# Moving the rests of w_up's pairs from POOL to DVE, a wide unit 13, the last norm's rows made twice, and the second tile of x on ACT's queue

## The chip, the core and the metric

The kernel runs on one core of a Trainium2 chip. The core has five engines with instruction streams of their own: TensorE (PE: matrix products, with weight loads shown apart as PEld), VectorE (DVE), ScalarE (ACT), GpSimd (POOL) and SyncE (SP, which here only issues transfers). They work from SBUF (on-chip memory) and PSUM (the banks into which PE writes) and wait for one another by semaphores. The metric is the device time of one launch in microseconds, as the median of several runs. The kernel before takes 1517.14 us (three runs, 1516.60 to 1517.77).

## The reference, cut to what matters

A decoder trunk of two layers on 512 tokens of 1024 channels. Each layer has a norm, one wide projection, two attention mixers, an output projection, a second norm and a squared-ReLU MLP; a final norm follows the last layer. The change lies in the MLP's first product, in the very first norm's input, and in the final norm.

```python
def rmsnorm(x, g):
    xf = x.astype(jnp.float32)
    y = xf * lax.rsqrt(jnp.mean(xf * xf, axis=-1, keepdims=True) + RMS_EPS)
    return (y * g.astype(jnp.float32)).astype(x.dtype)

def hybrid_layer(x, norm_mix, w_in, ..., norm_mlp, w_up, w_down):
    h = rmsnorm(x, norm_mix)
    proj = h @ w_in
    ...
    x = x + mixed @ w_out
    h = rmsnorm(x, norm_mlp)
    return x + jnp.square(jax.nn.relu(h @ w_up)) @ w_down

def reference(x, ..., norm_final):
    for l in range(DEPTH):
        x = hybrid_layer(x, ...)
    return rmsnorm(x, norm_final)
```

All is float32, with D_MODEL = 1024, SEQ = 512, D_FF = 4096.

## The kernel before

**Precision.** Each operand of a product is kept as a pair: a part `h` in the type fp32r, made by a copy on ACT, and a rest `lo = value - h`, a subtraction (TENSOR_TENSOR) that DVE or POOL makes. A product is then three matmuls: h by h, h by rest, rest by h (lines 243 to 245, and in the same way 358 to 360 in the first projection, 1529 ff. and 1543 ff. in the MLP). The channels lie on the 128 partitions and the tokens along the free dimension, so x is eight tiles `x[0]` to `x[7]` of 128 x 512.

**The head.** `token_proj` (line 332) takes x tile by tile as it arrives. `first_u` (1197) issues the load of tile k and makes `u` from it: `make_u` (265) scales the tile by the norm's gain on ACT (line 268) and takes the rest on DVE (269). `sumsq` (272) squares the tile on ACT (279) and adds it to a running sum `acc` on POOL, the last one on DVE (289). The weights wva are split by `convert` (ACT line 217, DVE line 218). `rstd` (296) then sums over the partitions with PE (303), takes the reciprocal root in a few small steps (306 to 318) and spreads the result over all partitions with PE again (323), from where it is copied to SBUF (327). A table load (ACT_TABLE_LOAD, line 294) stands before the last square.

**The MLP.** `mlp` (1087) makes eight of w_up's 32 column blocks plainly (`PLAIN`); the other 24 go in twelve units g = 4 to 15, a pair of column blocks each, by a scheme of Strassen's kind with seven products for four rows and columns of blocks (`unit`, 1547). A unit makes its products one after another into PSUM banks. Between them `next(conv, None)` converts the next unit's operands (ACT line 1521, DVE line 1522; sums of weights on DVE at 1517 and 1519, and by accumulating transfers that POOL issues at 1494 and 1503), and `between()` puts in a `down` (1104): four steps of w_down's product (twelve matmuls, 243 to 245), which DVE adds to x (1108). The seven results are combined by ACT copies (1606 to 1616) and by DVE (1620, 1624, 1628), and `halves` (1637) adds two halves on DVE (1640). `act` (1643) makes the activation of each of the unit's two blocks: relu and square on ACT (1652, 1653), its fp32r part on ACT (1654), and its rest (1655), on POOL for all but the last two of each layer's blocks. PE waits for the results of all of these: a bank can be filled again only when its reader has taken it (1108, 1628 and others), and a `down` reads activations.

A unit's products are made wide or slim. In the wide form (`product`, 1537) x's two parts stand beside each other, so the first matmul of each step has a moving side of 512 columns and the second one of 256; in the slim form (`narrow`, 1526) there are three matmuls of 256. Units 13 to 15 are slim. A slim unit also skips `halves`: it combines its results at 1587, 1591 and 1595.

**The tail.** The last product is followed by `out` (1165), once for each half of the tokens. The second half has nothing behind it: `rstd`, then eight products of x with the spread-out row, six on DVE (from PSUM) and two on POOL (from the copy R in SBUF), in the order written in `write`, and their stores on SP's queue or, for POOL's two, on ACT's.

**What sets the order.** Each engine runs its own stream in order. The program text gives the dependencies and the interleaving shown above; the order of instructions within an engine's stream is settled when the program is built, and it can shift with a small edit. A wait at the head of a stream holds all that stands behind it.

Of the kernel before, what the change touches and what calls it, by code (L numbers as in the profile page):

```python
# [11 lines left out]
F32 = mybir.dt.float32  # L12
F32R = mybir.dt.float32r
AF = mybir.ActivationFunctionType
OP = mybir.AluOpType
# [128 lines left out]
class Body:  # L144
# [151 lines left out]
    def rstd(self, acc, tags=("O", "O"), wait=iter(()), exp=True, copy=True, R=None):  # L296

        nc = self.nc
        n = acc[0].shape[-1] // 128
        ps = self.p(tags[0])  # L300
        for i, t in enumerate(acc):
            for b in range(n):
                nc.tensor.matmul(ps[:, 2 * b:2 * b + 2], t[:, b * 128:(b + 1) * 128], self.ones2,
                                 start=i == 0 and b == 0, stop=i == len(acc) - 1, skip_group_check=True)
        v, s, y, z = (self.t("s4", [128, NB], name=k)[:, :n] for k in "vsyz")
        nc.vector.tensor_scalar(v, ps[:, 0:2 * n:2], 1.0 / D, 1e-6, op0=OP.mult, op1=OP.add)
        if not copy:

            for _ in range(3):
                nc.tensor.matmul(ps[:, 128:256], v[:, :1].to_broadcast([128, 128]), self.ident, start=True, stop=True)  # L310
        nc.scalar.activation(s, v, AF.Sqrt)
        if exp:
            self.table(AF.Exp, s)
        nc.vector.reciprocal(y, s)
        nc.vector.tensor_mul(z, y, y)
        nc.vector.scalar_tensor_tensor(z, z, -0.5, v, op0=OP.mult, op1=OP.mult)
        rc = self.t("g4", [128, NB], name="rcol")[:, :n]
        nc.vector.scalar_tensor_tensor(rc, z, 1.5, y, op0=OP.add, op1=OP.mult)
        for _ in range(2):
            next(wait, None)  # L320
        ps = self.p(tags[1])[:, :128 * n]
        for b in range(n):
            nc.tensor.matmul(ps[:, b * 128:(b + 1) * 128], rc[:, b:b + 1].to_broadcast([128, 128]), self.ident,
                             start=True, stop=True)
        if R is None:
            R = self.t("r", [128, T], name="R")[:, :128 * n]
        nc.scalar.copy(R, ps)
        return (R, rc) if copy else (ps, R)

# [755 lines left out]
    def mlp(self, l, x, u, acc, gm):  # L1087
# [35 lines left out]
        for j in range(self.PLAIN):  # L1123
            ps = self.bank()
            w = self.weights(a["wup"][l, j].rearrange("p k c -> p (k c)"))
            run(self.gemm(ps, w, 0, u))
            if R is None and j == 0:
                pend.append(ps)
                continue
            if R is None:  # L1130
                R, _ = self.rstd(acc, (self.turn_tag(), self.turn_tag()))
                prep = S.prepare(R)
                for p in pend:
                    act(p)
            act(ps)
            for _ in range(3):
                next(prep, None)
# [27 lines left out]
    def out(self, x, f, acc, wait):  # L1165

        nc, a = self.nc, self.a
        n = T // 2
        tags = [self.turn_tag() for _ in range(2)]
        R, r = self.rstd(acc, tags, wait=wait, exp=False, copy=f == 0)  # L1170

        def write():

            for k, w in ((0, 2), (6, 1), (2, 2), (7, 1), (4, 1), (5, 1)):
                y = self.t("t2", [128, 2, n], name="y")[:, :w]
                for j in range(w):
                    pool = f and k > 5
                    (nc.gpsimd if pool else nc.vector).tensor_tensor(
                        y[:, j], x[k + j][:, f * n:(f + 1) * n], r if pool else R, op=OP.mult)
                    if j + 1 < w:  # L1180
                        yield
                (nc.scalar if f and k > 5 else nc.sync).dma_start(a["yT"][f, :, k:k + w], y)
                yield

        return write()
# [10 lines left out]

    def first_u(self, u, k):
        x = self.x0[:, k]
        self.nc.sync.dma_start(x, self.a["xT"][k])
        u.append(self.make_u(x, self.gain[:, :8], k))  # L1200
        return x

# [33 lines left out]
class Strassen:  # L1236
# [310 lines left out]
    def unit(self, g, D, n, acts):  # L1547
        b, nc = self.b, self.nc
        V, A = nc.vector, nc.scalar
        conv = self.convert(g + 1)  # L1550
        places = iter({1: (1,), 2: (0, 1), 3: (0, 1, 2), 4: (0, 1, 2, 3)}.get(n, ()))
        place = [next(places, None)]
        here = iter(range(4))

        def between():
            if next(here) == place[0]:
                place[0] = next(places, None)
                next(D)()

        slim = g > 12  # L1560

        def product(i, onto=None):
            ps = (b.bank()[:, :256] if slim else b.bank()) if onto is None else onto
            (self.narrow if slim else self.product)(ps, g, i, onto is None)
            return ps

        tag = "kd" if g > 13 else "o2"
        if slim:
            m = product(0)
            z = b.t("zc", [128, 2, 512], name="z")  # L1570
            lo, hi = slice(0, 256), slice(256, 512)
            A.copy(z[:, 1, lo], m)
            next(conv, None)
            p5 = product(1)
            A.copy(z[:, 0, hi], p5)
            next(conv, None)
            between()
            product(2, m)
            A.activation(z[:, 1, hi], m, AF.Copy, scale=-1.0)
            next(conv, None)  # L1580
            p4 = product(3)
            A.copy(z[:, 0, lo], p4)
            next(conv, None)
            between()
            product(4, m)
            v = z[:, 0].rearrange("p (k c) -> p k c", k=2)
            V.tensor_tensor(v, v, m[:, None, :].to_broadcast([128, 2, 256]), op=OP.add)
            self.act(z[:, 0], acts, tag)
            next(conv, None)
            p2 = product(5)  # L1590
            V.tensor_tensor(z[:, 1, lo], p2, z[:, 1, lo], op=OP.subtract)
            next(conv, None)
            between()
            product(6, p5)
            V.tensor_tensor(z[:, 1, hi], z[:, 1, hi], p5, op=OP.subtract)
            self.c.append(z)
            self.act(z[:, 1], acts, tag)
            next(conv, None)
            between()
            for _ in conv:  # L1600
                pass
            return
        m = product(0)
        y = b.t("zz", [128, 2, 512], name="y")
        z = b.t("zz" if g < 12 else "zc", [128, 2, 512], name="z")
        A.copy(y[:, 0], m)
        next(conv, None)
        p5 = product(1)
        A.copy(z[:, 1], p5)
        next(conv, None)  # L1610
        between()
        product(2, m)
        A.activation(y[:, 1], m, AF.Copy, scale=-1.0)
        next(conv, None)
        p4 = product(3)
        A.copy(z[:, 0], p4)
        next(conv, None)
        between()
        product(4, m)
        V.tensor_tensor(z, z, m[:, None, :].to_broadcast([128, 2, 512]), op=OP.add)  # L1620
        self.act(self.halves(z, z[:, 0]), acts, tag)
        next(conv, None)
        p2 = product(5)
        V.tensor_tensor(y[:, 0], p2, y[:, 0], op=OP.subtract)
        next(conv, None)
        between()
        product(6, p5)
        V.tensor_tensor(y[:, 1], y[:, 1], p5, op=OP.subtract)
        if g > 11:
            self.c.append(z)  # L1630
        self.act(self.halves(y, y[:, 0] if g < 12 else z[:, 1]), acts, tag)
        next(conv, None)
        between()
        for _ in conv:
            pass
# [7 lines left out]
    def act(self, c, acts, tag):  # L1643

        b, nc = self.b, self.nc
        if tag == "kd":
            if len(acts) % 2 == 0:
                self.late = b.t("kd" if len(acts) == 30 else "a4", [128, 4, T], F32R, name="ohl")
            h, lo = (self.late[:, len(acts) % 2 * 2 + i] for i in range(2))
        else:  # L1650
            h, lo = b.two(tag, "o")
        nc.scalar.activation(c, c, AF.Relu)
        nc.scalar.activation(c, c, AF.Square)
        nc.scalar.copy(h, c)
        (nc.vector if len(acts) > 29 else nc.gpsimd).tensor_tensor(lo, c, h.bitcast(F32), op=OP.subtract)  # L1655
        acts.append((h, lo))


# [34 lines left out]
```

## Time and profile before

| | |
|---|---|
| median of three runs | 1517.14 us |
| profiled execution, its own time | 1516.51 us |
| its span in the profile | 1514.7 us |
| granted TensorE clock, mean | 0.998 |
| POOL busy | 190.2 us |
| where w_up's units run (span) | 490 to 720 us and 1240 to 1470 us |

All times in the profile are microseconds from the start of the span, or ns where that is said. A group's row names the line of the kernel, the engine, the operation, what is written and read (buffer numbers left out) with shapes and types, and the count; "[0.52 <-POOL o L1655]" behind a row means that the engine had stood idle for 0.52 us before it, and that POOL's instruction at line 1655 on a tile `o` ended the wait. `ps_S`, `ps_O`, `ps_mm` and `ps_PT` are PSUM banks. Matmuls are pipelined: a row's duration includes the tail that overlaps the next one, so the distance between starts, not the duration, is what one costs.

### The profile page before, as it was taken

To read this page: it belongs to the slowest core of one execution; us is meant where nothing else is said; L and a number is where in the kernel's file an instruction comes from. 1 tells how busy PE (TensorE), PEld (TensorE's weight loads), DVE (VectorE), ACT (ScalarE), POOL (GpSimd) and SP (SyncE) were. 2 spreads that over 40 slices of the span, in tenths; PEclk is the share of its full clock that TensorE was granted. 3 is DMA by queue.
4 is the path that set the end of the run, shared out by engine and by line. 5 is a ranking of instruction groups with operands and counts; after the bars stand their busy time and mean duration, and the time that the engine had idled before them with its cause. 6 is when DMAs were issued, how large, how long until landed. Compare 5 with 4: busy or idle time off the path is not lost.

```text
span 1514.7 us, 22040 instructions
## 1 busy us (share of the span) xinstructions
PE 1500.4 (99%) x7970; PEld 1271.5 (84%) x7970; DVE 1153.3 (76%) x2211; ACT 835.9 (55%) x1592; POOL 190.2 (13%) x195
## 2 busy tenths in 40 slices
PE   9999999999999999999999999999999999999998
PEld 8888888888888888889988788888888888888997
DVE  5678978777478777878846789787674978888785
ACT  6465656554454656555545556565544635656555
POOL 4010000000300222221220000000012002222211
PEclk9999999999999999999999999999999999999999
DMA  7654422227325454553266543222363245555422
GB/s 262 173 164 127 142 70 70 70 70 234 109 96 146 130 149 133 146 143 122 84 197 181 154 125 99 84 70 71 123 205 98 88 142 153 150 141 141 126 77 64
DMA packets 70461, 194.12 MB, mean 128 GB/s; under 512 B 8880, under 2 KB 10288, under 8 KB 70352
## 3 DMA queue, kind: packets, MB, share of 16 engines
q1 hardware_dynamic: 57248, 169.36, 36.1%
q0 software_dynamic: 9216, 16.78, 6.4%
q10 hardware_dynamic: 3888, 6.58, 1.2%
q8 instruction: 63, 1.03, 0.3%
q14 instruction: 46, 0.38, 0.1%
HBM read 148.58 MB, written 4.19 MB: 101 GB/s over the span
## 4 chain that ended last, share of the span: by engine, by line
PE 89%; DVE 5%; ACT 2%; issue 2%; POOL 0%; DMA 0%; SPq 0%; DVEq 0%; ACTq 0%; POOLq 0%
PE ps_mm L243 11%; PE ps_mm L244 11%; PE ps_mm L245 11%; PE ps_PT L243 3%; PE ps_PT L244 3%; PE ps_PT L245 3%; PE ps_O L1543 3%; PE ps_S L1543 3%; PE ps_O L602 2%; PE ps_PT L576 2%; PE ps_S L243 2%; PE ps_S L244 2%; PE ps_S L245 2%; PE ps_S L551 2%; PE ps_O L243 2%; PE ps_O L244 2%
## 5 line engine op out<-in xcount | busy, mean ns | idle before, releaser
L217 ACT CAST wh<-raw 128x1024 fp32r<-128x1024 f32 (+2 forms) x177 | 182.0, 1028 | 238.1 <-PE ps_mm L244 75.8
L218 DVE TENSOR_TENSOR wl<-raw,wh 128x1024 fp32r<-128x1024 f32 (+2 forms) x177 | 218.0, 1232 | 38.1 <-ACT wh L217 37.6
L243 PE MATMUL ps_mm<-u,wh 128*128 128x512 f32 x512 | 205.1, 401 | 0.0
L244 PE MATMUL ps_mm<-u,wh 128*128 128x512 f32 x512 | 201.7, 394 | 0.0
L245 PE MATMUL ps_mm<-u,wl 128*128 128x512 f32 x512 | 201.7, 394 | 0.0
L1522 DVE TENSOR_TENSOR s<-raw,s 128x512 fp32r<-128x512 f32 x168 | 137.8, 833 | 30.4 <-ACT s L1521 29.3
L1521 ACT CAST s<-raw 128x512 fp32r<-128x512 f32 x168 | 102.6, 618 | 49.4 <-PE ps_O L1543 13.3
L1494 POOL DMA_DIRECT2D raw<-raw x28 | 24.6, 880 | 758.4 <-PE ps_PT L576 477.9
L245 PEld LDWEIGHTS ps_mm<-u,wl 128*128 128x128 f32 x512 | 96.2, 188 | 20.0
L243 PEld LDWEIGHTS ps_mm<-u,wh 128*128 128x128 f32 x512 | 96.6, 189 | 19.3 <-DVE E L452 0.8
L244 PEld LDWEIGHTS ps_mm<-u,wh 128*128 128x128 f32 x512 | 96.4, 188 | 16.9 <-issue 0.4
L243 PE MATMUL ps_mm<-o,wh 128*128 128x512 f32 x256 | 101.5, 396 | 1.3 <-DVE x L1108 1.3
L244 PE MATMUL ps_mm<-o,wh 128*128 128x512 f32 x256 | 100.3, 392 | 0.5 <-POOL o L1655 0.5
L245 PE MATMUL ps_mm<-o,wl 128*128 128x512 f32 x256 | 100.3, 392 | 0.0
L580 ACT CAST pth<-ps_PT 128x384 fp32r<-128x384 f32 (+1 forms) x96 | 49.0, 512 | 64.7 <-PE ps_PT L576 64.6
L538 DVE CUSTOM_DVE_ANT_0 E<-ps_S,ct 128x384 f32<-128x384 f32 (+3 forms) x112 | 57.3, 514 | 30.4 <-PE ps_S L551 29.6
L539 ACT ACTIVATE E<-E,tiny 128x384 f32<-128x384 f32 (+3 forms) x112 | 65.6, 586 | 20.0 <-DVE tiny L538 19.8
L581 DVE TENSOR_TENSOR ptl<-ps_PT,pth 128x384 fp32r<-128x384 f32 (+1 forms) x96 | 56.8, 599 | 14.2 <-ACT pth L580 12.9
L243 PEld LDWEIGHTS ps_mm<-o,wh 128*128 128x128 f32 x256 | 48.2, 188 | 12.0 <-DVE x L1108 2.3
L245 PEld LDWEIGHTS ps_mm<-o,wl 128*128 128x128 f32 x256 | 48.2, 188 | 10.3
L244 PEld LDWEIGHTS ps_mm<-o,wh 128*128 128x128 f32 x256 | 48.2, 188 | 9.8 <-POOL o L1655 0.8
L244 PE MATMUL ps_PT<-o,wh 128*128 128x512 f32 x136 | 53.2, 391 | 0.5 <-POOL o L1655 0.5
(455 smaller groups left out, 3771.7 us busy)
## 6 DMA issues: line engine op xcount, KB each, us to landing
raw<-wb SPq DMA_DIRECT2D x64, 512.0 KB, 3.2
raw<-wup SPq DMA_DIRECT2D x64, 512.0 KB, 3.5
raw<-wd SPq DMA_DIRECT2D x48, 512.0 KB, 3.5
raw<-raw POOLq DMA_DIRECT2D x64, 256.0 KB, 3.4
w<-w SPq DMA_DIRECT2D x32, 256.0 KB, 5.0
kda<-hla SPq DMA_DIRECT2D x32, 256.0 KB, 3.6
q2a<-hla SPq DMA_DIRECT2D x64, 128.0 KB, 2.3
raw<-wo SPq DMA_DIRECT2D x16, 512.0 KB, 3.6
```

What stands on the lines that cost most here:

```text
L217: nc.scalar.copy(h[:, :n], raw[:, :n])
L218: nc.vector.tensor_tensor(lo[:, :n], raw[:, :n], h[:, :n].bitcast(F32), op=OP.subtract)
L243: mm(ps, h[:, c], xh, start=start and i == 0, stop=False)
L244: mm(ps, h[:, c], xl, start=False, stop=False)
L245: mm(ps, lo[:, c], xh, start=False, stop=stop and i == ks - 1)
L538: nc.vector.tensor_tensor_reduce(e, ps, self.mask[:, T - n:], -1.0, BIG, OP.add, OP.min, mx)
L539: nc.scalar.activation(e, e, AF.Exp, bias=mx, scale=-1.0, accum_out=un["sm"][:, i:i + 1])
L580: nc.scalar.copy(h[:, e, :n], ps[:, :n])
L581: nc.vector.tensor_sub(lo[:, e, :n], ps[:, :n], h[:, e, :n].bitcast(F32))
L1521: nc.scalar.copy(h, src)
L1522: nc.vector.tensor_tensor(lo, src, h.bitcast(F32), op=OP.subtract)
L1543: mm = lambda o, w, x, **kw: self.nc.tensor.matmul(o, w, x, skip_group_check=True, **kw)
```

## The change

Four edits, independent of one another in the program's text:

- `act`: the rest of every activation of the units is made on DVE (44 instructions move from POOL: 22 in each layer).
- `unit`: unit 13 uses the wide form; only 14 and 15 are slim.
- `rstd` and `out`: the rows that spread the last norm's factor are made once for each tag after the first. `out` asks for two sets in the second half (`2 + f` tags): DVE reads the first set, ACT copies the second for POOL. The order of the output's tiles changes from (0, 1), 6, (2, 3), 7, 4, 5 to 0, 6, (1, 2), 7, (3, 4), 5.
- `first_u`: tile 1 of x is loaded by a transfer on ACT's queue; the others stay on SP's.

```diff
-        ps = self.p(tags[1])[:, :128 * n]
-        for b in range(n):
-            nc.tensor.matmul(ps[:, b * 128:(b + 1) * 128], rc[:, b:b + 1].to_broadcast([128, 128]), self.ident,
-                             start=True, stop=True)
+        rows = [self.p(tag)[:, :128 * n] for tag in tags[1:]]
+        for ps in rows:
+            for b in range(n):
+                nc.tensor.matmul(ps[:, b * 128:(b + 1) * 128], rc[:, b:b + 1].to_broadcast([128, 128]), self.ident,
+                                 start=True, stop=True)
         if R is None:
             R = self.t("r", [128, T], name="R")[:, :128 * n]
         nc.scalar.copy(R, ps)
-        return (R, rc) if copy else (ps, R)
+        return (R, rc) if copy else (rows[0], R)
...
-        tags = [self.turn_tag() for _ in range(2)]
+        tags = [self.turn_tag() for _ in range(2 + f)]
...
-            for k, w in ((0, 2), (6, 1), (2, 2), (7, 1), (4, 1), (5, 1)):
+            for k, w in ((0, 1), (6, 1), (1, 2), (7, 1), (3, 2), (5, 1)):
...
-        self.nc.sync.dma_start(x, self.a["xT"][k])
+        (self.nc.scalar if k == 1 else self.nc.sync).dma_start(x, self.a["xT"][k])
...
-        slim = g > 12
+        slim = g > 13
...
-        (nc.vector if len(acts) > 29 else nc.gpsimd).tensor_tensor(lo, c, h.bitcast(F32), op=OP.subtract)
+        nc.vector.tensor_tensor(lo, c, h.bitcast(F32), op=OP.subtract)
```

## The prediction

> **What bounds the kernel now.** I read the page first: busy times of the engines, then its chain of waits.
>
> ```profile
> span 1514.7 us, 22040 instructions
> PE 1500.4 (99%) x7970; PEld 1271.5 (84%) x7970; DVE 1153.3 (76%) x2211; ACT 835.9 (55%) x1592; POOL 190.2 (13%) x195
> PE 89%; DVE 5%; ACT 2%; issue 2%; POOL 0%; DMA 0%; SPq 0%; DVEq 0%; ACTq 0%; POOLq 0%
> ```
>
> TensorE (PE) is busy 1500.4 of 1514.7 us, so the change can win only where PE stands still, or by giving PE less to do. Next I asked the view of waits what PE waited for in the two stretches in which w_up's products run, first 490 to 720 us (four rows), then 1240 to 1470 us (four rows). Columns: total us, times, longest.
>
> ```profile
> PE ps_mm L243 <- DVE x L1108: 0.9, 2, 0.5
> PE ps_mm L244 <- POOL o L1655: 0.5, 1, 0.5
> PE ps_S L1543 <- DVE y L1628: 0.4, 2, 0.2
> PE ps_S L1529 <- DVE x L1108: 0.3, 1, 0.3
> ...
> PE ps_PT L244 <- POOL o L1655: 0.5, 1, 0.5
> PE ps_mm L243 <- DVE x L1108: 0.5, 1, 0.5
> PE ps_S L1529 <- DVE z L1595: 0.4, 1, 0.4
> PE ps_S L1543 <- DVE y L1628: 0.2, 1, 0.2
> ```
>
> Ten stalls, 2.1 + 1.6 = 3.7 us. Two of them wait for the instruction that moves (L1655), seven for VectorE (DVE) in wide units or beside them, one for L1595 in the old narrow unit 13. The idle time understates a stall, as two rows of PE's timeline show:
>
> ```profile
> 528.34 0.51 PE L1543 MATMUL ps_PT<-t,s 128*128 128x512 f32 x2
> 529.37 0.50 PE L244 MATMUL ps_mm<-o,wh 128*128 128x512 f32 x1 [0.52 <-POOL o L1655]
> ```
>
> Two matmuls of L1543 (one wide, one half as wide) take a quarter of the 1.40 us that eight take (row at 650.86 below): 0.35 us. L244 could thus have started at 528.69; it started at 529.37, 0.68 us late, where the idle time says 0.52. With 0.16 more for each, the ten cost 3.7 + 1.6 = 5.3 us. That is all this part can give back on PE.
>
> How full DVE is, from the view by stretches (us of the stretch, then PE, PEld, DVE, ACT, POOL busy) at the densest 30 us:
>
> ```profile
> 650.00:680.00 30.00, 30.00 (x197) 27.43 (x196) 25.00 (x36) 19.33 (x36) 8.57 (x7) 1.00 0.55 142
> ```
>
> 25.0 of 30 us: 5 us free, and at a granted clock of 1.00.
>
> **Part 1: the rests (L1655) from POOL to DVE.**
>
> ```profile
> L1655 POOL TENSOR_TENSOR o<-z,o x24: 1286/1296/2258, 509.5 to 1423.0; 128x512 fp32r<-128x512 f32 x24
> L1655 POOL TENSOR_TENSOR o<-y,o x16: 1286/1584/1620, 512.5 to 1388.0; 128x512 fp32r<-128x512 f32 x16
> L1655 POOL TENSOR_TENSOR ohl<-z,ohl x4: 1287/1346/1521, 687.1 to 1440.4; 128x512 fp32r<-128x512 f32 x4
> L1655 DVE TENSOR_TENSOR ohl<-z,ohl x4: 683/689/692, 705.9 to 1458.8; 128x512 fp32r<-128x512 f32 x4
> L1522 DVE TENSOR_TENSOR s<-raw,s 128x512 fp32r<-128x512 f32 x168 | 137.8, 833 | 30.4 <-ACT s L1521 29.3
> ```
>
> 44 instructions leave POOL (1.29 us at least) and come to DVE, where the same form takes 0.689 us: 44 x 0.689 = 30.3 us more for DVE, 15.2 a layer. Against it stands L1522: the same form with the same two SBUF inputs, yet 833 ns in the mean. Why shows in the timelines (DVE, then ACT, then POOL):
>
> ```profile
> 558.00 0.69 DVE L1108 TENSOR_TENSOR x<-x,ps_O 128x512 f32<-128x512 f32 x1 [0.50 <-PE ps_O L245]
> 558.91 1.37 DVE L1522 TENSOR_TENSOR s<-raw,s 128x512 fp32r<-128x512 f32 x1 [0.21 <-ACT s L1521]
> 565.55 2.34 DVE L1522 TENSOR_TENSOR s<-raw,s 128x512 fp32r<-128x512 f32 x1 [1.13 <-ACT s L1521]
> ...
> 557.73 0.62 ACT L1654 CAST o<-z 128x512 fp32r<-128x512 f32 x1
> ...
> 558.44 1.29 POOL L1655 TENSOR_TENSOR o<-z,o 128x512 fp32r<-128x512 f32 x1 [2.03 <-ACT o L1654]
> 565.75 1.57 POOL L1655 TENSOR_TENSOR o<-y,o 128x512 fp32r<-128x512 f32 x1
> ```
>
> L1522 takes 1.37 and 2.34 us exactly where POOL runs L1655 (to 559.73 and 567.32), and ends 0.55 and 0.57 us after POOL does; L1108, which reads PSUM, keeps 0.69. So POOL's rest holds DVE up. Over all 168, 168 x (0.833 - 0.689) = 24.2 us would go with the last L1655 on POOL: DVE's net load grows by 30.3 - 24.2 = 6.1 us, 3 a layer spread over some 220 us. The 5 free us in 30 cover that.
>
> What counts is the order. In the changed program DVE's new rests stand mostly just ahead of the L1522 that stands before L1628 or L1108. At 558: L1654 ends at 558.35, so the rest can run on DVE from 558.6 to 559.2, L1522 to 559.8, where it ended at 560.28 before; L1628 behind it starts 0.4 us earlier, and its stall (0.2 idle + 0.16) goes. At 565: L1522 ends at 567.89 now; rest plus L1522 from 565.55 need 1.38 less 0.16 of overlap, to 566.8; L1108 comes 1.1 us earlier and the stall at 568.5 (one of the two of the first row) goes. At 529: DVE is free for the rest at about 528.1 and ends it near 528.8, POOL ended it at about 529.3; 0.1 to 0.2 us of the 0.68 stays. Going through the queue of both stretches this way, with ACT and PE held at their times, some L1108 come 0.3 to 0.7 us later where PE has that much slack; no place turned into a new stall. I leave 0.4 us of the 5.3: **-4.9 us**. Bounds: -5.3 if all go; 0 if L1522 is slow for another reason, and then new waits come (third rival).
>
> The Trainium skill ("SBUF — State Buffer", section "SBUF: two separate sides") says the shared port pair goes to whichever of the two starts first, for its whole instruction. The row at 565.55 differs: DVE began 0.2 us ahead of POOL and still took 2.34 us. By the rule that stall is not POOL's and its 0.5 us would stay; by the row it goes.
>
> **Part 2: unit 13 in wide products** (slim from g > 13). On PE:
>
> ```profile
> 650.86 1.56 PE L1543 MATMUL ps_S<-b,s 128*128 128x512 f32 x8
> 652.26 1.60 PE L1529 MATMUL ps_O<-b,s 128*128 128x256 f32 x12
> 653.70 1.60 PE L1529 MATMUL ps_mm<-t,s 128*128 128x256 f32 x12
> ...
> L1640 DVE TENSOR_TENSOR z<-z x18: 679/682/686, 506.3 to 1397.1; 128x512 f32<-128x512 f32 x18
> ```
>
> A wide product runs from 650.86 to 652.26, 1.40 us; a narrow one 1.44. Seven products, two layers: 14 x 0.04 = **-0.5 us**. DVE gets two L1640 of 0.68 us in a unit and wider forms of three others: estimated 2.4 us a layer, into a stretch with 5 free (the 650 to 680 row), so nothing on the path; without that cover, up to 2.4 a layer. The wait for L1595 goes with the narrow unit, and L1628 takes its place.
>
> **Part 3: the last norm's rows.** For the second half R's rows are made twice, for DVE and for the copy that POOL reads.
>
> ```profile
> 1506.93 0.71 PE L323 MATMUL ps_O<-tiny 128*128 128x128 f32 x4
> 1507.68 0.37 ACT L327 COPY R<-ps_O 128x256 f32<-128x256 f32 x1 [1.59 <-PE ps_O L323]
> 1508.09 2.07 DVE L1178 TENSOR_TENSOR y<-x,ps_O 128x256 f32<-128x256 f32 x6 [1.21 <-ACT R L327]
> 1508.13 1.41 POOL L1178 TENSOR_TENSOR y<-x,R 128x256 f32<-128x256 f32 x2 [6.15 <-ACT R L327]
> ```
>
> DVE's products wait for ACT's copy although they read the same rows as the copy does. With rows of their own they can start when the first four passes end, about 1507.69: 1508.09 - 1507.69 = **-0.4 us** for the six and the store behind the last one. ACT's copy and POOL's two products come later, by at most the 0.71 of a second four passes: POOL would end by 1509.54 + 0.71 = 1510.25 instead of 1509.54, DVE at 1509.76 instead of 1510.16. At that bound POOL sets the end and the part costs 0.1 (1510.25 against 1510.16); passes that follow one another overlap, so I take half, POOL at 1509.9, and leave -0.4. Bounds +0.1 to -0.4. The stores on SP's queue go out as 1, 2, 2 and 1 tiles where they were 2, 2, 1 and 1: four as before, with the single last tile unchanged.
>
> **Part 4: the second tile of x on ACT's queue.** ACT issues it while it waits for the gain (1.07 us idle below), ahead of its first u, so nothing behind it is late; SP has one issue less. The tile may land earlier; but the built program also has another order on ACT: the square of tile 2 now stands behind all u's up to the last tile's.
>
> ```profile
> 3.76 0.72 ACT L268 ACTIVATE u<-x,tiny 128x512 fp32r<-128x512 f32 x1 [1.07 <-DMA tiny<-gain]
> 13.09 0.63 ACT L279 ACTIVATE sq<-x 128x512 f32<-128x512 f32 x1
> 13.79 1.88 POOL L289 TENSOR_TENSOR acc<-sq,acc 128x512 f32<-128x512 f32 x1 [1.16 <-ACT sq L279]
> 25.71 0.69 DVE L289 TENSOR_TENSOR acc<-sq,acc 128x512 f32<-128x512 f32 x1 [2.26 <-ACT sq L279]
> 28.36 0.95 PE L303 MATMUL ps_O<-tiny,acc 128*128 128x2 f32 x8
> ...
> 12.46 0.92 SPq L1199 DMA_DIRECT2D x<-xT  x2
> DMA to landing us min/median/max: 3.5/4.6/5.7
> ```
>
> The square of tile 2 starts at 13.09, its sum at 13.79, and five sums later the last acc ends at 25.71 + 0.69 = 26.40, and PE asks for it at 28.36: slack 1.96. The last tile's DMA is issued at about 12.9 (second of the two at 12.46) and lands 3.5 to 4.6 us on: 16.4 to 17.5. Its u takes 0.7 us, so that square moves to 17.1 to 18.2: 4.0 to 5.1 later. The five steps now take 25.71 - 13.79 = 11.9, 2.4 each; at their shortest, square 0.63 + sum 1.3 and two handovers of 0.07, they take 2.06, 1.6 us less in all, because the long sums (1.88) fell beside DVE's u's, which now stand ahead of them. PE then waits at L303 between 4.0 - 1.96 - 1.6 = 0.4 and 5.1 - 1.96 = 3.1 us. I take +0.8, near the low end. Whatever an early second tile gains before 28 us is swallowed by this wait, so its gain is 0: **+0.8 us**.
>
> **Sum**, against the profiled execution's own time 1516.51 (span 1514.7 and 1.8 around it): -4.9 - 0.5 - 0.4 + 0.8 = -5.0, 1511.5. It lies 0.63 under the median 1517.14, so the forecast for the median is **1512.1 us**.
>
> **Rivals.**
> *The head takes it back.* Same as above, but L303 waits its 3.1 us: 1512.1 + 2.3 = 1514.4. For it: six waits in a chain of engines. Against: the sums run without DVE beside them.
>
> *The moved work does not free PE.* The stalls stay where they are since L1108 and L1628 are late by 0.69 us of rest instead of 0.7 of slowed L1522: 1517.1 - 0.5 - 0.4 + 0.8 = 1517.0. For it: 30.3 and 24.2 us nearly cancel. Against: the two places walked above.
>
> *DVE becomes the waiting engine: slower.* DVE runs in order, and each new rest waits there for ACT's L1654, with L1108 and L1628, which PE needs, behind it. It decides where L1654 ends later than DVE gets to the rest. At 558 ACT ended 0.3 us ahead of it. If in every second of the 20 wide units it costs one stall of the present size (5.3 / 10 = 0.53), and the old stalls stay: 1517.0 + 10 x 0.53 = 1522.3.
>
> **How the numbers follow.** Forecast 0.55, head 0.19, no relief 0.13, slower 0.13. A measurement of this kernel tells about 0.2% from no change, 3 us: faster is under 1514.1, slower over 1520.2. The forecast's own range is 1510 to 1514, all faster; the head's waits from 0.8 to 3.1 put 0.07 of its 0.19 there: 0.62 faster. The rest of the head, the case without relief and 0.01 of the slower one make 0.26 within; 0.12 slower. The range for all: from 1517.14 - 5.3 - 0.5 - 0.4 = 1510.9, with 1 us for L303 and for DVE's new order, 1509.9, up to 1516.8, which leaves out the slower case and the upper part of the one without relief.
>
> **What would show it.** Right: no wait of PE for L1655, and L1108 and L1628 gone from PE's waits in both stretches; L1522 near 0.69 in the mean; DVE's busy time up by 6 + 5 us and POOL's down by some 60; the y's 0.4 us earlier after the last L323; L303 in the head waiting 0.4 to 3 us for the last acc. Wrong: new waits of PE for L1655 on DVE or for L1108, L1522 still over 0.8 us, or a first stall near 29 us of more than 3.

## The result, and the profile after

| | before | after |
|---|---|---|
| median | 1516.70 us (6 runs, 1516.32 to 1517.77) | 1511.05 us (6 runs, 1510.32 to 1512.07) |
| profiled execution, its own time | 1516.51 us | 1510.32 us |
| its span | 1514.7 us | 1508.5 us |

The ratio is 0.9962, with a 95% interval of 0.9949 to 0.9975: the medians differ by 5.65 us, 0.4%. The forecast was 1512.1.

In the profile of the changed kernel the line numbers from 323 on are one higher: L1656 is the rest that was L1655, L1523 was L1522, L1109 was L1108, L1629 was L1628. Its page: the span, the busy times, the chain of waits, and DVE's group of conversions (columns: busy us, mean ns, idle before).

```profile
span 1508.5 us, 21855 instructions
PE 1497.6 (99%) x7918; PEld 1268.5 (84%) x7918; DVE 1150.6 (76%) x2259; ACT 837.3 (56%) x1592; POOL 129.0 (9%) x151
PE 93%; DVE 3%; issue 2%; POOL 1%; ACT 1%; DMA 0%; POOLq 0%; SPq 0%; DVEq 0%; ACTq 0%
L1523 DVE TENSOR_TENSOR s<-raw,s 128x512 fp32r<-128x512 f32 x168 | 113.3, 688 | 33.4 <-ACT s L1522 32.3
```

PE now makes up 93% of the chain and DVE 3% (89 and 5 before). The same 168 conversions take 113.3 us instead of 137.8. DVE took over 44 subtractions, and is still busy 2.7 us less than before.

The view by stretches over the two w_up stages (columns: us of the stretch, then PE, PEld, DVE, ACT, POOL busy, the granted clock, DMA's share and GB/s), first before, then after:

```profile
490.00:720.00 230.00, 227.91 (x1249) 195.97 (x1249) 181.75 (x241) 135.71 (x234) 49.68 (x45) 1.00 0.50 137
1230.00:1470.00 240.00, 238.32 (x1304) 205.23 (x1303) 187.54 (x251) 137.62 (x237) 50.76 (x46) 1.00 0.49 135
```
```profile
490.00:720.00 230.00, 230.00 (x1248) 198.11 (x1247) 182.88 (x271) 137.59 (x236) 19.92 (x23) 1.00 0.49 138
1230.00:1470.00 240.00, 240.00 (x1310) 207.12 (x1309) 190.00 (x284) 139.70 (x240) 21.93 (x26) 1.00 0.47 132
```

PE's busy time now fills both stretches. The view of waits, which lists idle times from 0.15 us on, has none of the ten stalls left for PE and no new one. One of the places walked in the prediction, in DVE's timeline of the changed kernel:

```profile
558.75 0.69 DVE L1109 TENSOR_TENSOR x<-x,ps_O 128x512 f32<-128x512 f32 x1 [0.57 <-PE ps_O L245]
559.36 0.69 DVE L1656 TENSOR_TENSOR o<-z,o 128x512 fp32r<-128x512 f32 x1
559.96 0.69 DVE L1523 TENSOR_TENSOR s<-raw,s 128x512 fp32r<-128x512 f32 x1
560.56 0.68 DVE L1629 TENSOR_TENSOR y<-y,ps_PT 128x512 f32<-128x512 f32 x1
```

From the start of L1109 to that of L1629 it is 1.81 us, with the rest in between; before it was 2.20 us (558.00 to 560.20) without it. That is the 0.4 us of the prediction.

In the head there are two waits where there was one. First PE's timeline of the changed kernel, then DVE's and POOL's around the second wait:

```profile
28.94 1.05 PE L303 MATMUL ps_O<-tiny,acc 128*128 128x2 f32 x8 [1.18 <-DVE acc L289]
...
38.30 0.40 PE L360 MATMUL ps_mm<-wl,u 128*128 128x288 f32 x1 [0.80 <-DVE wl L218]
...
36.51 3.48 DVE L218 TENSOR_TENSOR wl<-raw,wh 128x576 fp32r<-128x576 f32 x2 [0.75 <-ACT wh L217]
...
36.35 3.03 POOL L901 TENSOR_TENSOR crs<-crs,ct 128x512 f32<-128x512 f32 x2 [4.54 <-DMA crs<-rope]
```

The same two engines in the kernel before:

```profile
35.83 0.76 DVE L218 TENSOR_TENSOR wl<-raw,wh 128x576 fp32r<-128x576 f32 x1 [0.74 <-ACT wh L217]
...
36.85 3.06 POOL L900 TENSOR_TENSOR crs<-crs,ct 128x512 f32<-128x512 f32 x2 [5.74 <-DMA crs<-rope]
```

L303 starts at 28.94 instead of 28.36. That alone would cost 0.6 us. But DVE's L218 now comes 0.7 us later (36.51, not 35.83) and POOL's rope products, two instructions with two SBUF inputs each, 0.5 us sooner (36.35, not 36.85). Before, the first L218 was done when POOL began. Now it begins behind POOL, two L218 of 0.76 us take 3.48, and PE waits again.

In the tail, PE, then ACT, then DVE of the changed kernel; then the start of the same chain before:

```profile
1500.49 0.93 PE L310 MATMUL ps_PT<-tiny 128*128 128x128 f32 x6 [0.25 <-DVE tiny L306]
1502.06 0.61 PE L324 MATMUL ps_mm<-tiny 128*128 128x128 f32 x4
...
1502.70 0.37 ACT L328 COPY R<-ps_mm 128x256 f32<-128x256 f32 x1 [2.03 <-PE ps_mm L324]
...
1502.26 2.08 DVE L1179 TENSOR_TENSOR y<-x,ps_O 128x256 f32<-128x256 f32 x6 [0.80 <-PE ps_O L324]
```
```profile
1505.91 0.93 PE L310 MATMUL ps_PT<-tiny 128*128 128x128 f32 x6 [0.25 <-DVE tiny L306]
```

DVE starts 1.77 us after L310 instead of 2.18 (1505.91 to 1508.09), and no longer behind ACT's copy.

### The profile page after: what moved, and what is told of

It is laid out like the page before. It is cut to its first block, busy times and chain, and to the rows that moved or that the text cites. A ratio compares the mean times of both kernels' runs of the same rounds, so it can differ in the third digit from the quotient of the medians.

```text
span 1508.5 us, 21855 instructions
## 1 busy us (share of the span) xinstructions
PE 1497.6 (99%) x7918; PEld 1268.5 (84%) x7918; DVE 1150.6 (76%) x2259; ACT 837.3 (56%) x1592; POOL 129.0 (9%) x151
## 4 chain that ended last, share of the span: by engine, by line
PE 93%; DVE 3%; issue 2%; POOL 1%; ACT 1%; DMA 0%; POOLq 0%; SPq 0%; DVEq 0%; ACTq 0%
PE ps_mm L243 11%; PE ps_mm L244 11%; PE ps_mm L245 11%; PE ps_O L1544 3%; PE ps_S L1544 3%; PE ps_PT L1544 3%; PE ps_mm L1544 3%; PE ps_PT L243 3%; PE ps_PT L245 3%; PE ps_PT L244 3%; PE ps_O L603 2%; PE ps_S L243 2%; PE ps_S L245 2%; PE ps_PT L577 2%; PE ps_S L244 2%; PE ps_O L243 2%
## 5 line engine op out<-in xcount | busy, mean ns | idle before, releaser
L218 DVE TENSOR_TENSOR wl<-raw,wh 128x1024 fp32r<-128x1024 f32 (+2 forms) x177 | 214.4, 1211 | 41.4 <-ACT wh L217 40.4
L244 PE MATMUL ps_mm<-u,wh 128*128 128x512 f32 x512 | 201.8, 394 | 0.0
L1523 DVE TENSOR_TENSOR s<-raw,s 128x512 fp32r<-128x512 f32 x168 | 113.3, 688 | 33.4 <-ACT s L1522 32.3
L1522 ACT CAST s<-raw 128x512 fp32r<-128x512 f32 x168 | 102.3, 619 | 48.6 <-PE ps_O L1544 17.5
L244 PEld LDWEIGHTS ps_mm<-u,wh 128*128 128x128 f32 x512 | 96.4, 188 | 16.8 <-issue 0.4
L244 PE MATMUL ps_mm<-o,wh 128*128 128x512 f32 x256 | 100.1, 391 | 0.0
L244 PEld LDWEIGHTS ps_mm<-o,wh 128*128 128x128 f32 x256 | 48.2, 188 | 9.1 <-DVE o L494 0.4
```

The costliest lines, as they stand in the source:

```text
L218: nc.vector.tensor_tensor(lo[:, :n], raw[:, :n], h[:, :n].bitcast(F32), op=OP.subtract)
L244: mm(ps, h[:, c], xl, start=False, stop=False)
L1522: nc.scalar.copy(h, src)
L1523: nc.vector.tensor_tensor(lo, src, h.bitcast(F32), op=OP.subtract)
```

## The experiments

All medians are of four runs or more; "before" ran beside each on the same chip and lay between 1516.40 and 1516.85.

| kernel | median, us | ratio to before, interval |
|---|---|---|
| changed kernel | 1511.05 | 0.9962 [0.9949, 0.9975] |
| changed, rests back on POOL | 1522.17 | 1.0041 [1.0028, 1.0053] |
| changed, second tile on SP's queue | 1508.97 | 0.9952 [0.9939, 0.9964] |
| changed, unit 13 slim | 1511.17 | 0.9966 [0.9953, 0.9978] |
| changed, one set of rows | 1511.19 | 0.9967 [0.9956, 0.9979] |
| changed, POOL repeats the subtractions | 1532.02 | 1.0100 [1.0086, 1.0114] |
| changed, POOL fills instead | 1510.35 | 0.9957 [0.9944, 0.9969] |
| changed, head's sums on DVE | 1509.38 | 0.9951 [0.9938, 0.9963] |
| changed, rope products on DVE | 1510.41 | 0.9963 [0.9949, 0.9976] |
| changed, both of these | 1508.92 | 0.9950 [0.9936, 0.9964] |
| before, unit 13 wide alone | 1520.70 | 1.0026 [1.0016, 1.0036] |
| before, rests on DVE alone | 1510.02 | 0.9958 [0.9946, 0.9971] |
| changed, old order of the stores | 1511.39 | 0.9965 [0.9951, 0.9978] |

### The rests back on POOL

```diff
-        nc.vector.tensor_tensor(lo, c, h.bitcast(F32), op=OP.subtract)
+        (nc.vector if len(acts) > 29 else nc.gpsimd).tensor_tensor(lo, c, h.bitcast(F32), op=OP.subtract)
```

> The changed kernel (1511.05 us) with the 44 rests back on POOL, all else as changed. Theory (POOL's rests slow DVE's L1523 and so hold PE): PE waits for L1656 and for L1109 and L1629 return in both stretches, L1523's mean goes from 0.688 back to 0.80 to 0.84 us, and the time rises by 4 to 5.5 us, to 1515 to 1516.5. Rival (the gain is that of the wide unit and of the ends, the rests only changed place): at most 1512.5.

It took 1522.17 us, 5.3 more than before and 11.1 more than the changed kernel; twice the most that the theory had, and far from the rival's 1512.5. The waits are back as expected (L1656, L1629 and L1109, L1523 at 0.820 us), but one of them is far larger. First two of these rows, then DVE and POOL ahead of the large wait, then PE:

```profile
PE ps_mm L244 <- POOL o L1656: 0.5, 1, 0.5
L1523 DVE TENSOR_TENSOR s<-raw,s 128x512 fp32r<-128x512 f32 x168 | 135.3, 820 | 29.9 <-ACT s L1522 28.7
...
671.12 3.12 DVE L1641 TENSOR_TENSOR z<-z 128x512 f32<-128x512 f32 x1
...
670.90 2.79 POOL L1656 TENSOR_TENSOR o<-z,o 128x512 fp32r<-128x512 f32 x2
...
684.68 0.80 PE L243 MATMUL ps_PT<-o,wh 128*128 128x512 f32 x1 [2.59 <-DVE x L1109]
685.27 0.63 PE L244 MATMUL ps_PT<-o,wh 128*128 128x512 f32 x1
685.70 0.63 PE L245 MATMUL ps_PT<-o,wl 128*128 128x512 f32 x1
```

An addition of 0.68 us (L1641) lasts 3.12 beside two rests on POOL, in the unit that became wide; DVE is full from there on, and PE waits 2.59 us for L1109. Then something comes that no wait explains: the matmuls behind it start 0.43 us apart instead of 0.23. The view by stretches has the reason in its column after POOL's, the granted clock:

```profile
676.00:682.00 6.00, 6.00 (x40) 5.39 (x39) 6.00 (x9) 4.90 (x11) 1.72 (x2) 1.00 0.37 105
682.00:685.00 3.00, 0.41 (x2) 0.32 (x2) 2.97 (x4) 2.12 (x5) 1.02 (x1) 0.84 0.59 235
685.00:690.00 5.00, 5.00 (x13) 3.84 (x13) 1.76 (x4) 0.22 (x1) 0.90 (x1) 0.50 0.62 150
```

PE ran 5 us at half its clock after the wait, some 2.4 us more (twelve matmuls at 0.2 us). This execution is the longest of the five (1524.02 us, mean clock 0.995). The median one had 0.998, where the changed kernel's six runs have 0.997 to 0.999, and still took 11.1 us more; so the slow clock is not needed for most of the loss. What follows: the rests are the large term, and rests on POOL and a wide unit 13 together cost far more than the 4 to 5.5 us that was expected of the rests.

### Each of the two alone

```diff
-        slim = g > 12
+        slim = g > 13
```

> The kernel before with unit 13 in wide products and nothing else changed. Theory (with the rests on POOL the wide unit's extra DVE work meets slowed DVE instructions, and the wait for L1109 near 680 us, 2.6 us and 5 us at half the granted clock behind it, comes from the two together): 3 to 6 us more than before, 1520 to 1523. Rival (the 1522.2 with the rests back on POOL came from the other edits): 0 to 0.7 us less than before.

1520.70 us, 4.1 more than before. PE's waits in the profiled execution, and the stretch behind the longest:

```profile
PE ps_PT L243 <- DVE x L1108: 2.2, 1, 2.2
PE ps_mm L243 <- DVE x L1108: 1.7, 3, 0.8
...
680.00:690.00 10.00, 8.60 (x49) 7.58 (x50) 7.67 (x14) 4.91 (x9) 2.27 (x3) 1.00 0.62 178
```

The wait for L1108 is where it was expected, 2.2 us long. The clock stayed at 1.00 in this execution, which took 1518.65, the shortest of nine; the others took 1519.9 to 1521.9, at mean clocks down to 0.996. So the wait is shown; the slow clock behind it is shown in the profiled execution of the first experiment only.

```diff
-        (nc.vector if len(acts) > 29 else nc.gpsimd).tensor_tensor(lo, c, h.bitcast(F32), op=OP.subtract)
+        nc.vector.tensor_tensor(lo, c, h.bitcast(F32), op=OP.subtract)
```

> The kernel before with the 44 rests on DVE and nothing else changed. Theory (the rests are worth all of the stalls of the two stretches, seen ones and those too short for the view of waits): 6 to 7 us less, 1509.9 to 1510.9. Rival (they are worth the 4.9 us of the forecast, and the wide unit adds to it): 1511.5 to 1512.3.

1510.02 us, 6.6 less than before. DVE's busy time fell to 1146.5, from 1153.3, with 44 more instructions:

```profile
PE 1497.8 (99%) x7970; PEld 1271.7 (84%) x7970; DVE 1146.5 (76%) x2255; ACT 835.3 (55%) x1592; POOL 130.6 (9%) x151
```

By the medians the rests alone are worth a microsecond more than all four edits; the runs overlap (1509.81 to 1512.13, and 1510.32 to 1512.07), so that microsecond is not shown by this pair. The rests are worth at least about as much as the whole.

### What on POOL slows DVE

```diff
-        self.gain = self.tiny[:, 640:680]
+        self.gain = self.tiny[:, 640:680]; self.scratch = self.sb.tile([128, T], F32, name="scratch", tag="scratch", bufs=1)
...
-        nc.vector.tensor_tensor(lo, c, h.bitcast(F32), op=OP.subtract)
+        nc.vector.tensor_tensor(lo, c, h.bitcast(F32), op=OP.subtract); len(acts) > 29 or nc.gpsimd.tensor_tensor(b.scratch, c, h.bitcast(F32), op=OP.subtract)
```

> The changed kernel, and in addition POOL does each of the 44 subtractions a second time into a tile that nobody reads. Nothing on PE, DVE or ACT waits for POOL's copy. Theory (a subtraction on POOL slows DVE's instructions with two SBUF inputs while it runs): L1523's mean goes from 0.688 to 0.80 us or more, DVE's busy time rises by 20 to 40 us, PE waits for L1109 and L1629 come back, and the time is 4 to 15 us longer, 1515 to 1526. Rival (PE waited because POOL's own result was late): nothing changes, 1510.5 to 1511.5.

1532.02 us: 21 more than the changed kernel, over the expected 4 to 15. DVE's busy time is 1191.0, 40 more. The page's group of L1523, two of the rows of line 1656 (min/median/max ns; they cover 24 of the 44 rests), and PE's longest waits in the first stage:

```profile
L1523 DVE TENSOR_TENSOR s<-raw,s 128x512 fp32r<-128x512 f32 x168 | 121.8, 747 | 16.9 <-ACT s L1522 16.2
...
L1656 POOL TENSOR_TENSOR scratch<-z,o x24: 1287/1602/1798, 512.8 to 1437.4; 128x512 f32<-128x512 f32 x24
L1656 DVE TENSOR_TENSOR o<-z,o x24: 677/1684/2148, 512.8 to 1437.8; 128x512 fp32r<-128x512 f32 x24
...
PE ps_S L1530 <- DVE x L1109: 2.5, 1, 2.5
PE ps_O L1530 <- DVE z L1592: 1.8, 1, 1.8
```

L1523 missed its 0.80, at 0.747 (9.9 us in all): most of the loss, 23.7 us, fell on the rest itself. Where it starts when POOL's twin does it takes 1.68 us in the median of these 24, instead of 0.69; of all its rows 22 took over 1 us, and the others kept 0.69. In two places the granted clock was 0.50 for 3.4 us (from 31.3 and 1434.2 us), which explains about 3.4 of the 21 us at most. No engine waits for POOL's twin here, so a wait of PE needs no late result of POOL. In the kernel before, two of the ten stalls (L244 for L1655) did wait for POOL's own result, so there the rival holds for these two.

```diff
...
-        nc.vector.tensor_tensor(lo, c, h.bitcast(F32), op=OP.subtract)
+        nc.vector.tensor_tensor(lo, c, h.bitcast(F32), op=OP.subtract); len(acts) > 29 or [nc.gpsimd.tensor_copy(b.scratch[:, :1], h[:, :1].bitcast(F32))] + [nc.gpsimd.memset(b.scratch, 0.0) for _ in range(3)]
```

> The changed kernel, and in addition POOL writes zeros three times over a tile that nobody reads, in place of each of the second subtractions: about as long, but with no SBUF input except one column per partition. Theory (it is POOL's reading of SBUF that holds DVE up): L1523's mean stays at 0.69 us and the time at 1511 to 1511.6. Rival (any work of POOL on SBUF does): L1523 at 0.80 or more and 1515 to 1526 us, as with the repeated subtractions.

1510.35 us, a little under the expected 1511 to 1511.6; its profiled span is that of the changed kernel, 1508.5 us. The same rows:

```profile
L1523 DVE TENSOR_TENSOR s<-raw,s 128x512 fp32r<-128x512 f32 x168 | 113.2, 687 | 33.5 <-ACT s L1522 32.7
...
L1656 POOL MEMSET scratch<- x132: 524/526/884, 511.7 to 1437.0; 128x512 f32 x132
L1656 DVE TENSOR_TENSOR o<-z,o x24: 680/685/693, 511.5 to 1418.9; 128x512 fp32r<-128x512 f32 x24
```

Three fills of 0.526 us, some 1.6 us each time, as long as the repeated subtraction: and L1523 keeps 0.687 us, the rest 0.685. Ahead of the fills stands a copy of one column of `h`. POOL's work that reads two tiles slows DVE's instructions; its work that writes, and reads one column, does not.

### The head

```diff
-        (self.nc.scalar if k == 1 else self.nc.sync).dma_start(x, self.a["xT"][k])
+        self.nc.sync.dma_start(x, self.a["xT"][k])
```

> The changed kernel with the second tile of x back on SP's queue, all else as changed. Theory (the squares' new order costs more than the early tile brings): PE's wait for the last acc in the head (1.2 us) goes, PE waits 0.6 us for the second u instead, and the time falls by 0.4 to 0.9 us, to about 1510.4. Rival (the early tile is a gain): 0.3 to 0.7 us more, about 1511.6.

1508.97 us (1508.53 to 1509.91, no overlap with the changed kernel's runs): 2.1 less, where 0.4 to 0.9 was expected. PE's wait for the second u is back, those for L303 and for L218 are gone:

```profile
9.06 0.50 PE L359 MATMUL ps_S<-wh,u 128*128 128x512 f32 x1 [0.64 <-ACT u L268]
```

The next two tell why it is more.

```diff
-                    self.acc = self.sumsq(x, self.acc, 2 * c + j == KT - 1)
+                    self.acc = self.sumsq(x, self.acc, True)
```

> The changed kernel with the head's sums of squares from the third tile on made by DVE in place of POOL. Theory (PE's wait at L303 is the chain of square and sum, 2.03 us a step with POOL's 1.3): a step takes 1.4 us, the last sum ends near 26 us, the wait of 1.2 us at L303 and the later wait for L218 near 37 us go, and the early second tile keeps its 0.7 us: 1.5 to 2.5 us less, 1508.5 to 1509.5. Rival (the squares start late since the last tile of x arrives late, and the steps don't matter): the wait stays, 1510.5 to 1511.3.

1509.38 us, 1.7 less. The last sum starts at 24.23 us, and L303 doesn't wait. A wait of 0.5 us for L218 near 36 us stayed: POOL's rope products run from 34.86 here.

```diff
-            nc.gpsimd.tensor_tensor(self.CRS[:, i], self.CRS[:, i], R, op=OP.mult)
+            nc.vector.tensor_tensor(self.CRS[:, i], self.CRS[:, i], R, op=OP.mult)
```

> The changed kernel with the two products of the rope tables (L901) on DVE in place of POOL. Theory (near 37 us L218 takes 2.7 us instead of 0.76 because POOL's L901 runs beside it): L218 takes 0.76 us again, PE's wait of 0.8 us for it falls below 0.4, and the time is 0.3 to 0.8 us less, 1510.2 to 1510.7. Rival (the weights' copies on ACT are late): the wait stays and the time grows by up to 0.7 us for DVE's extra work.

1510.41 us, 0.6 less. DVE's timeline has the products and the L218's in turn, each at its own length, and PE doesn't wait for them:

```profile
36.50 0.69 DVE L901 TENSOR_TENSOR crs<-crs,ct 128x512 f32<-128x512 f32 x1 [0.40 <-DMA crs<-rope]
37.11 0.75 DVE L218 TENSOR_TENSOR wl<-raw,wh 128x576 fp32r<-128x576 f32 x1
```

With both edits:

> The changed kernel with both the head's sums and the rope products on DVE. Theory (the two waits of the head are separate, and each goes with its POOL work): neither the wait at L303 nor the one for L218 near 36 us is left, and the time is 0.5 to 0.9 us under the 1509.4 of the sums alone: 1508.5 to 1508.9, about that of the kernel with the second tile on SP's queue (1508.97). Rival (the second wait hides another one behind it): 1509.2 to 1509.6.

1508.92 us, as expected: the two waits add. With the tile on SP's queue it was 1508.97; the two ways end alike, 2.1 us under the changed kernel and 0.5% under the kernel before. No gain of the early second tile shows in this comparison, but it is not a clean one, since the sums and the rope products moved too: L303 started at 28.36 us with the tile on SP's queue, at 27.87 with the sums on DVE, and at 28.64 with both on DVE.

### The wide unit, the rows and the order of the stores, taken back

```diff
-        slim = g > 13
+        slim = g > 12
```

> The changed kernel with unit 13 slim again, all else as changed. Theory (14 wide products save 0.04 us each on PE, nothing else is on the path): 0.5 us more, about 1511.6, up to 1512.0 if the wait for the slim unit's L1595 comes back. Rival (the wide unit's 2.4 us more on DVE cost PE as much as they save): no change or 0.3 us less.

1511.17 us, 0.1 more, which can't be told from the changed kernel; nor can it be told well from the 0.5 that was expected, with the changed kernel's runs 1.75 us apart. In its profile there is no wait of PE in the two stages either.

```diff
-        tags = [self.turn_tag() for _ in range(2 + f)]
+        tags = [self.turn_tag() for _ in range(2)]
```

> The changed kernel with one set of rows for the last norm, the output's new order kept. Theory (DVE's first product waits for ACT's copy of the same rows): the six products start 0.4 us later after the last L324, and the time rises by 0.4 us, to about 1511.45. Rival (POOL's two products and their stores end last, 0.3 us sooner with one set): 0.1 to 0.3 us less.

1511.19 us, also not to be told apart. In the profile the six products start 2.18 us after L310 again (1500.83 to 1503.01), as before, and behind ACT's copy.

```diff
-            for k, w in ((0, 1), (6, 1), (1, 2), (7, 1), (3, 2), (5, 1)):
+            for k, w in ((0, 2), (6, 1), (2, 2), (7, 1), (4, 1), (5, 1)):
```

> The changed kernel with the output's tiles stored in the order of before (pairs first, then two singles); the two sets of rows stay. Theory (with two singles at the end, SP's issue of the one before holds up the last store): from the start of the last L310 to the end of the span 8.2 to 8.5 us, against 8.01 in the changed kernel and 8.79 in the kernel before; the time 0.2 to 0.4 us longer, 1511.2 to 1511.5. Rival (the order does nothing, and the 0.4 us beyond the rows were chance of single executions): 7.95 to 8.1 us, 1510.9 to 1511.2.

1511.39 us, 0.3 more by the median, which can't be told apart. From the last L310 to the end of the span it is 8.29 us (1501.31 to 1509.6), inside the expected 8.2 to 8.5.

That whole stretch can't be compared between all kernels, because the granted clock differs in it. First the start of DVE's products with one set of rows (the kernel before this one) and with the old order; then the stretch around L310 with the clock, in the kernel with the old order and in the one with the rope products on DVE:

```profile
1503.01 2.07 DVE L1179 TENSOR_TENSOR y<-x,ps_O 128x256 f32<-128x256 f32 x6 [1.21 <-ACT R L328]
1503.08 2.08 DVE L1179 TENSOR_TENSOR y<-x,ps_O 128x256 f32<-128x256 f32 x6 [0.81 <-PE ps_O L324]
...
1500.00:1503.00 3.00, 2.66 (x22) 2.38 (x22) 0.81 (x5) 1.00 (x3) 0.00 (x0) 1.00 0.14 48
1500.00:1503.00 3.00, 2.97 (x14) 2.89 (x14) 1.25 (x6) 0.20 (x1) 0.00 (x0) 0.54 0.00 0
```

At the clock of 0.54 DVE's products start 2.36 us after L310, at 1.00 they start 1.77 after it. From the start of these products to the end of the span the clock matters little: 6.21 us in the kernel with 0.54, 6.24 in the changed one. There the four kernels with the old order (before, the two made from it, and this one) take 6.52 to 6.65 us, the ten with the new order 6.19 to 6.38. The order is thus worth 0.1 to 0.5 us in the profiled executions, 0.28 between this kernel and the changed one. SP's last issue shows where that comes from, in the changed kernel and then in this one:

```profile
1504.46 0.41 SPq L1183 DMA_DIRECT2D yT<-y  x1
1505.45 0.51 SPq L1183 DMA_DIRECT2D yT<-y  x1
```

With the new order it starts 2.20 us after DVE's first product (1502.26), with the old one 2.37 (1503.08), and it is 0.10 shorter. With the old order SP is busy with the issue before it until 2.27, though the last product is done at 2.08; that is the theory's reason. Where the clock stays at 1.00, the rows and the order bring the stretch from L310 to the end from 8.8 us to between 8.0 and 8.15.

## Why the prediction was right, and where it was off

**Direction and cause: right.** PE's standing still was what could be won, and it stood still because POOL's rests held DVE up. For eight of the ten stalls that is DVE slowed or filled; two waited for POOL's result itself. The repeated subtractions show that POOL's subtraction slows DVE and through it PE, and the fills show that writing alone does not. All ten stalls went, no wait of PE for L1656 on DVE came.

**The rests: -4.9 forecast, -6.6 measured (rests alone).** The term was mis-sized, and "that is all this part can give back on PE" was no bound. The 5.3 was built from the stalls that the view of waits lists, idle times of 0.15 us and longer, plus 0.16 each, and 0.4 was left to stay. I took the distances between the starts of neighbouring matmuls in the two stages and compared each with the median of its pair of forms. One more place 0.3 us late, and the many that are 0.02 to 0.15 us late, add up to 2.42 us before and 0.86 with the rests alone: 1.6 us that the view of waits doesn't list. With the ten stalls, all gone, that makes some 6.8; the medians have 6.6.

The rests' net load on DVE was off the same way: +6.1 us forecast, -6.8 measured (1153.3 to 1146.5). L1522 gave back what was counted (137.8 to 113.3 in the changed kernel, 24.5 for a forecast of 24.2). Not counted were L218, which took 5.8 us less with the rests alone, and the instructions at 1301 and 1303, 3.1 less. And a rest takes 0.60 us of DVE's time, not 0.69: in the timeline above the next instruction starts 0.60 us after it (559.36 and 559.96).

**The wide unit: -0.5 forecast, -0.1 measured, not to be told from zero nor well from 0.5.** That DVE's free time covers its 2.4 us a layer was right only because the rests had left POOL. With them there it costs 4.1 us. The prediction named that price ("without that cover, up to 2.4 a layer") but not what takes the cover away.

**The last norm's rows: -0.4 forecast.** DVE starts 0.41 us sooner after L310, as forecast, where the clock is 1.00. Two things were off. With POOL at 1509.9, as the prediction took it, POOL's product would have ended behind DVE's (1509.76), so its own numbers leave 0.3 and not 0.4. And the order of the stores was put at nothing ("four as before, with the single last tile unchanged"), while the profiled executions show 0.1 to 0.5 us for it. The medians can show neither.

**The second tile: +0.8 forecast, +2.1 measured.** The chain of squares and sums was right: step 2.03 us, last sum at 28.19, wait of 1.2 us at L303. What failed is the step "whatever an early second tile gains before 28 us is swallowed by this wait", as far as it takes L303 for the only place: behind it a second wait was missed. There DVE's L218 ran into POOL's rope products, the same contention as in part 1, at a place where it had not been looked for. With the sums on DVE 1.7 us of the 2.1 go, with the rope products there 0.6, with both all.

**The sum.** -6.6 - 0.1 + 2.1, and -0.1 to -0.8 for the tail (the last L310 to the end takes 7.97 to 8.74 us in the profiles with the whole new tail, 8.8 before), give -4.7 to -5.4; measured -5.65. Two errors of opposite sign, 1.7 in the rests and 1.3 in the head, brought 1512.1 near 1511.05; that they nearly cancel is luck.

**The rivals.** The slower one did not come. In the changed kernel DVE stands idle at a rest until ACT's L1655 ten times, 4.9 us in all, and PE has no wait from it. The kernel with the repeated subtractions is slower by another mechanism: there DVE itself is slowed. "The moved work does not free PE" falls with the rests alone. "The head takes it back" happened in part. The rule of the Trainium skill of who starts first ("SBUF — State Buffer", section "SBUF: two separate sides") left a stall of 0.5 us standing; it went, as by the row. In the kernel with the repeated subtractions the rule fits better:

```profile
528.16 0.69 DVE L1656 TENSOR_TENSOR o<-z,o 128x512 fp32r<-128x512 f32 x1
528.77 2.40 DVE L1523 TENSOR_TENSOR s<-raw,s 128x512 fp32r<-128x512 f32 x2
...
528.26 1.75 POOL L1656 TENSOR_TENSOR scratch<-z,o 128x512 f32<-128x512 f32 x1 [2.21 <-DVE y L1641]
```

DVE's rest, begun 0.1 us ahead of POOL, keeps its 0.69, and POOL takes 1.75 instead of 1.29; the next two on DVE take 2.40 instead of 1.3. The Trainium skill ("SBUF — State Buffer", section "Who interferes with whom") has it that a DVE instruction with two SBUF inputs contends with POOL's reading and not with its writing alone. The two experiments on POOL agree: 1.68 us in the median of the 24 rests shown, and 0.69.

## What to carry to other kernels

An engine with time to spare is not free: with 44 subtractions more on DVE, its busy time fell by 6.8 us, so beside POOL each of them had cost DVE more than it costs when DVE makes it, and in places PE waited for that. Before work is moved between two engines, compare the duration of the same form on one while the other runs and while it rests; and after a shift of even 0.7 us look for new overlaps of that pair everywhere, not only where it was changed. Take each edit of a bundle back once: of these four, one gave about all the gain, one took a third of that back, one brought a few tenths of a microsecond, and one pays at most half a microsecond and would have cost 4 us without the first.

## What the runs showed that had not been expected

A wait of PE can cost more than its length. After a wait of 2.59 us (rests back on POOL) the granted clock was 0.50 for 5 us and the matmuls of 512 columns lay 0.43 us apart instead of 0.23. In the kernel with the repeated subtractions it was 0.50 for 3.4 us behind a wait of 2.7 us. Behind the head's wait for L303, 1.0 us long in that kernel and 1.2 in the changed one, it was 0.50 in the first and 1.00 in the second. After 2.2 us in the profiled execution with the wide unit alone it stayed at 1.00. The Trainium skill ("TensorE: Matmul & The Clock Gate", section "Part 1: The HAM clock gate (the "warmup" mystery)") tells of a gate that halves the clock after an idle window of about 3.4 us, with 426.7 ns between cold matmuls of 512 columns. The distance agrees; the wait here was shorter than that window, and what decides was not tried.
